# A Mamba-2/GLA trunk: loads alone on the sync queue of the second part, stores on ScalarE's queue

## The chip, the cores and the metric

The kernel runs on one core of a Trainium2 chip. A core has five engines with instruction streams of their own: TensorE (PE, with its weight loads shown as PEld), VectorE (DVE), ScalarE (ACT), GpSimd (POOL) and SyncE (SP). SP and ScalarE can both issue DMAs; a DMA instruction stands in its engine's stream in order, and when it waits for a semaphore, what follows it in that stream waits too. The metric is the device time of one execution in microseconds (us); lower is better.

## The reference, cut to what matters

One decoder layer over 16 meta tokens and 2048 tokens, width 1024: a combined input projection, two branches (a Mamba-2 scan and gated linear attention), sigmoid gates that merge them, an output projection with a residual, and a final norm. The change touches only the last lines:

```python
    branches = jnp.stack([y_ssd.astype(y_gla.dtype), y_gla], axis=2)
    branch_proj = jnp.einsum('blnc,ncd->blnd', branches, w_branch)
    gates = jax.nn.sigmoid(merge_g.reshape(b, l, N_BRANCH, D_MODEL))
    merged = jnp.sum(gates * branch_proj, axis=2)
    return hres + jnp.einsum('bld,de->ble', merged, w_out)
...
    return rmsnorm(h, final_norm_w)[:, N_META:]
```

`merge_g` is the product of the normed input u with 2048 columns of the input weight.

## The kernel before, in words

The **first part** (to about 1556 us) works through four blocks of 512 tokens: projections, the scan, the attention. It leaves u and the two branch outputs y in DRAM, transposed. The **second part** (from about 1557 us) holds the large products: the gates, the two branch projections and the output projection. It works on units of 1024 tokens, so there are seven stages in this order: gate0, br00, br10, gate1, br01, br11, out (br*n**s* is branch *n* of unit *s*). A gate stage has 8 pairs of output tiles, a branch stage 4, the out stage 8.

Each stage multiplies 2x2 blocks in seven products instead of eight (Winograd's scheme). A product is 4 x 3 matmuls of 128x128 by 128x512: every fp32 operand is split into two fp32r parts, and three of the four cross products are added up. The order of products in a stage is written out in `order`: pairs are taken two at a time, and for each p of PS = (1, 2, 6, 7, 5, 3, 4) the product p of both. So 14 products make a round; the whole part has 280.

What belongs to a product:

- **A operands** (weights, or the merged tiles m in out): `load_a` fetches four raw tiles of a pair into `ar` buffers (8) by SP; GpSimd makes the sums (L887 to L890, the last into s4); `prep_a` (L896 ScalarE, L897 VectorE) splits one of the seven into an `a` buffer (7), five products ahead.
- **B operands** (u, y, the out weight, and sums of them): `load_b` fetches a raw tile into a `br` buffer (5) by SP (L870); `prep_b` (L875 ScalarE, L876 VectorE) splits it into `b1` to `b7`. The 28 tiles of the next stage are prepared from 12 products before the stage to 10 after its start.
- **Sums of B**: `make_sums` loads four quarter tiles (L76) into two `io` tiles, subtracts on GpSimd (L80) and stores two tiles (L83). Most are made beside the first part; those of the last unit's branches, 16 pieces, are `late` and made in the second part, one every 9 products from product 14, with their stores on SP.
- **Epilogues**: after products 1, 6 and 5, ScalarE copies the PSUM bank into `sn` (L913); product 6, 5 or 3 then goes on adding to that same bank. After products 2, 5, 4 and 3 `use` finishes an output tile. A gate tile is a tanh on ScalarE (L937), stored to g (L938). A branch tile loads its gate tile g into `io` (8 buffers, L948), adds the snapshot (L930), multiplies (L950); branch 0 stores the result to p (L952), branch 1 loads p (L955), adds (L956) and stores to m (L957). An out tile loads its rows of the input (L969), adds (L971), squares on ScalarE (L975); once both halves of a row are there the norm's factor is formed (L981, L982, L983 on GpSimd), both are scaled (L986) and stored (L987).

All loads and stores of the second part are issued by SP. In the first part TensorE and SP follow the order of the source (`tc.manual_schedule`); in the second part a planner places every engine's instructions, SP's and TensorE's too, by its own costs and the time at which it expects each to be ready. `at(pos, fn)` only says where in the source an action stands: after which product.

Of the kernel before, what the change touches and what calls it, by code (L numbers as in the profile page):

```python
# [40 lines left out]
def trunk_kernel(ctx: ExitStack, tc: tile.TileContext, xm, xmt, w_feat, w_tok, w_zm, w_br, w_o,  # L41
# [30 lines left out]
    def make_sums(pool, tag, nb, braw, sums, j, c, store):  # L72
# [6 lines left out]
        for o, x, y in ((b11, b12, b11), (b12, b22, b12), (b22, b22, b11), (b21, b21, b22)):  # L79
            nc.gpsimd.tensor_tensor(o, x, y, op=ALU.subtract)  # L80
        yield
        for dst, src in zip(sums, pair):
            store.dma_start(dst[j][:, :, cs], src)  # L83

# [770 lines left out]

    class Stage:
# [3 lines left out]
        def __init__(self, name, key, npairs, araw, use):  # L860
            self.name, self.npairs, self.araw, self.use = name, npairs, araw, use
            self.braw, self.sums = sums[key]
            self.b, self.braws, self.a, self.ps, self.snap = {}, {}, {}, {}, {}
# [15 lines left out]
        def load_a(self, n):  # L879
# [5 lines left out]
            a11, a21, a22, a12 = raw(0, 0), raw(1, 0), raw(1, 1), raw(0, 1)  # L885
# [14 lines left out]
        def product(self, n, p):  # L900
# [14 lines left out]
            if p == 2:  # L915
                self.use(n, 0, 0, ps, self.snap[n, 1])
            if p == 5:
                self.use(n, 1, 1, self.ps[n, "b"], self.snap[n, 5])
            if p == 4:
                self.use(n, 1, 0, ps, self.snap[n, 6])  # L920
            if p == 3:
                self.use(n, 0, 1, ps, None)
# [10 lines left out]
    def gate_stage(s):  # L933
        def use(n, i, t, ps, snap):
# [3 lines left out]
            nc.sync.dma_start(g_left[2 * s + t][2 * n + i], th)  # L938
# [5 lines left out]
    def branch_stage(s, nb):  # L944
        def use(n, i, t, ps, snap):
            d, b = 2 * n + i, 2 * s + t
            th = io()
            nc.sync.dma_start(th, g_left[b][nb * 8 + d])  # L948
            x = total(ps, snap)
            nc.vector.scalar_tensor_tensor(th, th, 1.0, x, op0=ALU.add, op1=ALU.mult)  # L950
            if nb == 0:
                nc.sync.dma_start(p_left[b][d], th)  # L952
            else:
                part = io()
                nc.sync.dma_start(part, p_left[b][d])  # L955
                nc.vector.tensor_tensor(part, part, th, op=ALU.add)  # L956
                nc.sync.dma_start(m_left[b][d // 4][:, d % 4], part)  # L957
# [3 lines left out]
                         "p (k c) -> p k c", c=P), use)  # L961

    def out_stage():
        fns, res, ssq = [], {}, {}

        def use(n, i, t, ps, snap):
            r0 = (2 * n + i) * P
            r = res[n, i, t] = io()
            nc.sync.dma_start(r, xm[META + r0:META + r0 + P, t * BLK:(t + 1) * BLK])  # L969
# [6 lines left out]
            if (n, i, 1 - t) in res:  # L976
# [7 lines left out]
                for hf in range(2):  # L984
                    o = res[n, i, hf]
                    nc.vector.scalar_tensor_tensor(o, o, q[:, 0:1], fns[hf], op0=ALU.mult, op1=ALU.mult)  # L986
                    nc.sync.dma_start(out[r0:r0 + P, hf * BLK:(hf + 1) * BLK], o)  # L987
# [3 lines left out]
                     use)  # L991
# [15 lines left out]
    AHEAD, LOAD = 5, 9  # L1007
# [120 lines left out]
```

## Time and profile before

| what | value |
|---|---|
| median of 3 runs (lowest to highest) | 2385.71 us (2382.58 to 2387.7) |
| the profiled execution: first to last instruction | 2382.4 us (the page gives no time around it) |
| TensorE busy | 2264.0 us (95%) |
| VectorE, ScalarE, GpSimd busy | 1571.8, 1187.5, 680.0 us |
| mean granted TensorE clock | 0.976 |
| SP's DMA queue, ScalarE's DMA queue | 452.66 MB, 63.06 MB |
| ScalarE's waits for br loads from 1560 us on, longest | 16.4 us (y), 13.6 us (out weight), 9.4 us (u) |

How to read the rows below. A timeline row has the start in us, the duration in us, the engine, the line of the kernel, the operation, out<-in by the names of the tiles (numbers left out), the shape, and in brackets the idle time before it with what ended it. SPq and ACTq are the instruction streams that issue DMAs. A row of waits reads "who waits <- for whom: us in total, times, longest us". A row of DMA issues has the count, the size and the median us from issue to landing. The window rows have start:end, length, then busy us and (instructions) of each engine. A busy PE overlaps its own matmuls (each row is 0.39 us long, they start 0.23 us apart), so the pace is read from starts.

### The profile page before, as it was taken

The page shows a single profiled execution, that of the slowest core. Times are in us where ns is not written, and L with a number is a line of the kernel's source. Part 1 is how long each engine was busy: PE and PEld are TensorE (multiplying, and loading weights), DVE is VectorE, ACT ScalarE, POOL GpSimd, SP SyncE. Part 2 cuts the span into 40 slices and gives each one's busy share as a digit, 9 for nine tenths or more (in the row PEclk, how much of TensorE's full clock was granted, in tenths as well). Part 3 has the DMA queues.
Part 4 walks back from the last instruction along what each step waited for, and adds up shares of the span by engine and source line. Part 5 has one row for each costly group of instructions (what it writes and reads, how often), then busy time and mean ns, then how long its engine had stood idle before and what let it go on. Part 6 is the DMA issues. An engine that isn't in the chain of part 4 may idle for free. (4 is left out here: it accounts for less than half of the span.)

```text
span 2382.4 us, 36669 instructions
## 1 busy us (share of the span) xinstructions
PE 2264.0 (95%) x12641; PEld 1970.8 (83%) x12641; DVE 1571.8 (66%) x2889; ACT 1187.5 (50%) x2764; POOL 680.0 (29%) x681
## 2 busy tenths in 40 slices
PE   6899999999999999999999999789989999998998
PEld 6889989888889988888989889668877788877786
DVE  4676665676675676676666655764757855786976
ACT  4665655465544455544455534364634445553443
POOL 3343433122222122321122100324433454332431
PEclk8999999999999999999999999789999999999999
DMA  8665875667786676786666654364777965787652
GB/s 271 213 209 193 293 240 190 225 201 235 245 276 184 215 220 220 258 267 199 208 213 212 205 167 143 131 217 136 263 248 264 313 198 173 251 264 225 231 177 106
DMA packets 301547, 518.07 MB, mean 217 GB/s; under 512 B 27696, under 2 KB 143664, under 8 KB 301360
## 3 DMA queue, kind: packets, MB, share of 16 engines
q1 hardware_dynamic: 231856, 452.66, 58.2%
q10 hardware_dynamic: 69504, 63.06, 8.0%
q8 instruction: 99, 1.62, 0.3%
q14 instruction: 88, 0.72, 0.1%
HBM read 368.42 MB, written 147.19 MB: 216 GB/s over the span
## 5 line engine op out<-in xcount | busy, mean ns | idle before, releaser
L177 PE MATMUL pj<-u,whl 128*128 128x512 f32 (+1 forms) x1184 | 447.4, 378 | 9.3 <-ACT g_all L420 3.3
L179 PE MATMUL pj<-u,whl 128*128 128x512 f32 (+1 forms) x1184 | 431.5, 364 | 0.8 <-POOL whl L165 0.8
L178 PE MATMUL pj<-u,whl 128*128 128x512 f32 (+1 forms) x1184 | 430.9, 364 | 0.0
L177 PE MATMUL pj<-whl,u 128*128 128x256 f32 (+1 forms) x992 | 289.9, 292 | 8.7 <-ACT u L282 6.1
L179 PE MATMUL pj<-whl,u 128*128 128x256 f32 (+1 forms) x992 | 284.1, 286 | 1.3 <-DVE u L284 1.3
L177 PE MATMUL psa<-b,a 128*128 128x512 f32 x640 | 255.5, 404 | 30.8 <-ACT sn L913 20.6
L178 PE MATMUL pj<-whl,u 128*128 128x256 f32 (+1 forms) x992 | 283.8, 286 | 0.7 <-POOL whl L165 0.5
L177 PEld LDWEIGHTS pj<-u,whl 128*128 128x128 f32 x1184 | 225.7, 191 | 47.1 <-ACT g_all L420 3.7
L179 PE MATMUL psa<-b,a 128*128 128x512 f32 x640 | 255.8, 400 | 2.3 <-DVE a L897 2.2
L179 PEld LDWEIGHTS pj<-u,whl 128*128 128x128 f32 x1184 | 225.2, 190 | 36.7 <-POOL whl L165 1.1
L178 PE MATMUL psa<-b,a 128*128 128x512 f32 x640 | 255.5, 399 | 0.0
L178 PEld LDWEIGHTS pj<-u,whl 128*128 128x128 f32 x1184 | 225.8, 191 | 33.2
L876 DVE TENSOR_TENSOR b<-br,b 128x512 fp32r<-128x512 f32 x196 | 160.8, 842 | 59.3 <-ACT b L875 58.9
L177 PEld LDWEIGHTS pj<-whl,u 128*128 128x128 f32 x992 | 191.0, 193 | 9.7 <-ACT u L282 6.6
L179 PEld LDWEIGHTS pj<-whl,u 128*128 128x128 f32 x992 | 191.2, 193 | 2.1 <-DVE u L284 2.1
L178 PEld LDWEIGHTS pj<-whl,u 128*128 128x128 f32 x992 | 191.1, 193 | 2.0 <-POOL whl L165 1.6
L897 DVE TENSOR_TENSOR a<-ar,a 128x512 fp32r<-128x512 f32 x160 | 136.2, 855 | 83.1 <-ACT a L896 82.6
L80 POOL TENSOR_TENSOR wr<-wr 128x256 f32<-128x256 f32 x80 | 66.2, 828 | 430.9 <-DMA wr<-y 173.0
L165 POOL TENSOR_TENSOR whl<-wr,whl 128x512 fp32r<-128x512 f32 (+1 forms) x100 | 132.7, 1334 | 191.6 <-ACT whl L164 166.3
L875 ACT ACTIVATE b<-br 128x512 fp32r<-128x512 f32 x196 | 119.8, 627 | 133.4 <-DMA br<-br_t 35.4
L177 PEld LDWEIGHTS psa<-b,a 128*128 128x128 f32 x640 | 124.9, 195 | 61.8 <-ACT sn L913 24.1
L462 DVE SCALAR_TENSOR_TENSOR acc<-cin,hcw,acc 128x512 f32<-128x512 f32 (+1 forms) x192 | 156.3, 814 | 26.8 <-ACT acc L458 26.1
(267 smaller groups left out, 5025.1 us busy)
## 6 DMA issues: line engine op xcount, KB each, us to landing
whl<-k_s SPq DMA_DIRECT2D x96, 512.0 KB, 4.5
whl<-k_g SPq DMA_DIRECT2D x96, 512.0 KB, 4.2
whl<-k_v SPq DMA_DIRECT2D x48, 512.0 KB, 3.9
whl<-k_z SPq DMA_DIRECT2D x36, 512.0 KB, 3.7
wr<-in_w_feat SPq DMA_DIRECT2D x64, 256.0 KB, 4.4
k_s<-whl SPq DMA_DIRECT2D x32, 512.0 KB, 3.5
cb<-cumd ACTq DMA_DIRECT2D x64, 256.0 KB, 5.7
y<-gg ACTq DMA_DIRECT2D x64, 256.0 KB, 4.6
```

The lines of the kernel that those rows point to most:

```text
L80: nc.gpsimd.tensor_tensor(o, x, y, op=ALU.subtract)
L165: nc.gpsimd.tensor_tensor(hl[:, 1], raw, hl[:, 0].bitcast(F32), op=ALU.subtract)
L177: nc.tensor.matmul(ps, sh, mh, start=first, stop=False, **kw)
L178: nc.tensor.matmul(ps, sh, ml, start=False, stop=False, **kw)
L179: nc.tensor.matmul(ps, sl, mh, start=False, stop=last, **kw)
L462: nc.vector.scalar_tensor_tensor(acc, cin[:, k:k + tt], hcw[:, ti, k:k + 1], acc, op0=ALU.mult, op1=ALU.add)
L875: nc.scalar.activation(t[:, 0], raw, AF.Copy)
L876: nc.vector.tensor_tensor(t[:, 1], raw, t[:, 0].bitcast(F32), op=ALU.subtract)
L897: nc.vector.tensor_tensor(t[:, 1], src, t[:, 0].bitcast(F32), op=ALU.subtract)
```

## The change

The second part's source now stands under `manual_schedule` for TensorE and SP, as the first part's does. Stores are collected (`late_store`) and issued by ScalarE's queue after a later product (`store_due`): one product later for epilogue tiles, two for the late sums. `fetch` loads the epilogue's tiles some products ahead of `use`: 3 for branch 0 and out, 2 for branch 1, where it loads g and p. The late sums stand at `spots`: eight pieces in each gate stage, from its product 9 on, one every 5 products, with no stage of their own in the branches. `load_a` stands 7.5 products before product 1 instead of 9, and loads a12 before a21; `load_b` stands 3.2 products before its `prep_b` instead of 4. The arithmetic and the buffers are the same.

```diff
@@ -78,9 +78,18 @@
         (b12, b11), (b22, b21) = [(t[:, 0], t[:, 1]) for t in pair]
         for o, x, y in ((b11, b12, b11), (b12, b22, b12), (b22, b22, b11), (b21, b21, b22)):
             nc.gpsimd.tensor_tensor(o, x, y, op=ALU.subtract)
+        if store is None:
+            for dst, src in zip(sums, pair):
+                late_store(dst[j][:, :, cs], src, 2)
+            return
         yield
         for dst, src in zip(sums, pair):
             store.dma_start(dst[j][:, :, cs], src)
+
+    stores, step_no = {}, [0]
+
+    def late_store(dst, src, lag=1):
+        stores.setdefault(step_no[0] + lag, []).append((dst, src))
 
     def new_sums(name):
         return [[wdram.tile([P, 2, BLK], F32, tag=f"{name}_t{i}_{j}", name=f"{name}_t{i}_{j}", bufs=1)
@@ -853,12 +862,21 @@
     m_left = [[wdram.tile([P, 4, BLK], F32, tag=f"m_{b}_{j}", name=f"m_{b}_{j}", bufs=1) for j in range(2)]
               for b in range(nblk)]
 
+    USES = {2: (0, 0), 5: (1, 1), 4: (1, 0), 3: (0, 1)}
+    store = late_store
+
+    def store_due(i):
+        for k in sorted(k for k in stores if k <= i):
+            for dst, src in stores.pop(k):
+                nc.scalar.dma_start(dst, src)
+
     class Stage:
 
 
 
-        def __init__(self, name, key, npairs, araw, use):
+        def __init__(self, name, key, npairs, araw, use, fetch=None, ahead=0):
             self.name, self.npairs, self.araw, self.use = name, npairs, araw, use
+            self.fetch, self.ahead = fetch, ahead
             self.braw, self.sums = sums[key]
             self.b, self.braws, self.a, self.ps, self.snap = {}, {}, {}, {}, {}
 
@@ -882,7 +900,7 @@
                 nc.sync.dma_start(t, self.araw(n, i, j))
                 return t
 
-            a11, a21, a22, a12 = raw(0, 0), raw(1, 0), raw(1, 1), raw(0, 1)
+            a11, a12, a21, a22 = raw(0, 0), raw(0, 1), raw(1, 0), raw(1, 1)
             s1, s2, s4 = [mk(rpl, [P, 4, P], F32, "as", bufs=6) for _ in range(3)]
             nc.gpsimd.tensor_tensor(s1, a21, a22, op=ALU.add)
             nc.gpsimd.tensor_tensor(s2, s1, a11, op=ALU.subtract)
@@ -912,14 +930,8 @@
                 sn = mk(opl, [P, BLK], F32, "sn", bufs=6)
                 nc.scalar.activation(sn, ps, AF.Copy)
                 self.snap[n, p] = sn
-            if p == 2:
-                self.use(n, 0, 0, ps, self.snap[n, 1])
-            if p == 5:
-                self.use(n, 1, 1, self.ps[n, "b"], self.snap[n, 5])
-            if p == 4:
-                self.use(n, 1, 0, ps, self.snap[n, 6])
-            if p == 3:
-                self.use(n, 0, 1, ps, None)
+            if p in USES:
+                self.use(n, *USES[p], self.ps[n, "b"] if p == 5 else ps, self.snap.get((n, {2: 1, 5: 5, 4: 6}.get(p))))
 
     def io():
         return mk(opl, [P, BLK], F32, "io", bufs=8)
@@ -935,45 +947,56 @@
             x = total(ps, snap)
             th = io() if snap is None else snap
             nc.scalar.activation(th, x, AF.Tanh, scale=0.5)
-            nc.sync.dma_start(g_left[2 * s + t][2 * n + i], th)
+            store(g_left[2 * s + t][2 * n + i], th)
 
         return Stage(f"gate{s}", ("g", s), 8,
                      lambda n, i, j: w_feat[T_GATE + 2 * n + i, :, j * BLK:(j + 1) * BLK].rearrange(
                          "p (k c) -> p k c", c=P), use)
 
     def branch_stage(s, nb):
+        got = {}
+
+        def fetch(n, i, t):
+            d, b = 2 * n + i, 2 * s + t
+            got[n, i, t] = tiles = [io() for _ in range(1 + nb)]
+            nc.sync.dma_start(tiles[0], g_left[b][nb * 8 + d])
+            if nb:
+                nc.sync.dma_start(tiles[1], p_left[b][d])
+
         def use(n, i, t, ps, snap):
             d, b = 2 * n + i, 2 * s + t
-            th = io()
-            nc.sync.dma_start(th, g_left[b][nb * 8 + d])
+            th, *part = got.pop((n, i, t))
             x = total(ps, snap)
             nc.vector.scalar_tensor_tensor(th, th, 1.0, x, op0=ALU.add, op1=ALU.mult)
             if nb == 0:
-                nc.sync.dma_start(p_left[b][d], th)
+                store(p_left[b][d], th)
             else:
-                part = io()
-                nc.sync.dma_start(part, p_left[b][d])
-                nc.vector.tensor_tensor(part, part, th, op=ALU.add)
-                nc.sync.dma_start(m_left[b][d // 4][:, d % 4], part)
+                nc.vector.tensor_tensor(part[0], part[0], th, op=ALU.add)
+                store(m_left[b][d // 4][:, d % 4], part[0])
 
         return Stage(f"br{nb}{s}", ("b", nb, s), 4,
                      lambda n, i, j: w_br[nb * 8 + 2 * n + i, :, j * BLK:(j + 1) * BLK].rearrange(
-                         "p (k c) -> p k c", c=P), use)
+                         "p (k c) -> p k c", c=P), use, fetch, 3 - nb)
 
     def out_stage():
-        fns, res, ssq = [], {}, {}
+        fns, res, ssq, done = [], {}, {}, set()
+
+        def fetch(n, i, t):
+            r0 = (2 * n + i) * P
+            res[n, i, t] = r = io()
+            nc.sync.dma_start(r, xm[META + r0:META + r0 + P, t * BLK:(t + 1) * BLK])
 
         def use(n, i, t, ps, snap):
             r0 = (2 * n + i) * P
-            r = res[n, i, t] = io()
-            nc.sync.dma_start(r, xm[META + r0:META + r0 + P, t * BLK:(t + 1) * BLK])
+            r = res[n, i, t]
+            done.add((n, i, t))
             x = total(ps, snap)
             nc.vector.scalar_tensor_tensor(r, x, 0.5, r, op0=ALU.mult, op1=ALU.add)
             if (n, i) not in ssq:
                 ssq[n, i] = mk(spl, [P, 2], F32, "ssf")
             jk = mk(spl, [P, BLK], BF16, "junk", bufs=1)
             nc.scalar.activation(jk, r, AF.Square, accum_out=ssq[n, i][:, t:t + 1])
-            if (n, i, 1 - t) in res:
+            if (n, i, 1 - t) in done:
                 while len(fns) < 2:
                     fns.append(mk(rpl, [P, BLK], F32, "br", bufs=5))
                     nc.sync.dma_start(fns[-1], fnw[:, (len(fns) - 1) * BLK:len(fns) * BLK].to_broadcast([P, BLK]))
@@ -984,11 +1007,11 @@
                 for hf in range(2):
                     o = res[n, i, hf]
                     nc.vector.scalar_tensor_tensor(o, o, q[:, 0:1], fns[hf], op0=ALU.mult, op1=ALU.mult)
-                    nc.sync.dma_start(out[r0:r0 + P, hf * BLK:(hf + 1) * BLK], o)
+                    store(out[r0:r0 + P, hf * BLK:(hf + 1) * BLK], o)
 
         return Stage("out", ("o",), seq // (2 * P),
                      lambda n, i, j: m_left[(2 * n + i) // 4][j][:, :, (2 * n + i) % 4 * P:((2 * n + i) % 4 + 1) * P],
-                     use)
+                     use, fetch, 3)
 
     stages = []
     for s in range(nsb):
@@ -1004,7 +1027,7 @@
         begins.append(len(order))
         for n in range(0, st.npairs, 2):
             order += [(st, n + i, p) for p in PS for i in range(2)]
-    AHEAD, LOAD = 5, 9
+    AHEAD, LOAD = 5, 7.5
     todo = {}
 
     def at(pos, fn):
@@ -1018,27 +1041,32 @@
         for q in range(28):
             p, j = PS[q // 4], q % 4
             pos = begins[si] - 12 + 0.8 * q if si else -0.99 + 0.2 * (q // 4) if q < 16 else 2 * (q // 4 - 4)
-            at(pos - (4 if si else 0.1), lambda st=st, p=p, j=j: st.load_b(p, j))
+            at(pos - (3.2 if si else 0.1), lambda st=st, p=p, j=j: st.load_b(p, j))
             at(pos, lambda st=st, p=p, j=j: st.prep_b(p, j))
     for i, (st, n, p) in enumerate(order):
+        if p in USES and st.fetch:
+            at(i - st.ahead, lambda st=st, n=n, p=p: st.fetch(n, *USES[p]))
+    for i, (st, n, p) in enumerate(order):
         at(i - AHEAD if i >= AHEAD else -0.95 + 0.1 * i, lambda st=st, n=n, p=p: st.prep_a(n, p))
-    i = 14
-    for key in late:
-        for j in range(4):
-            for c in range(2):
-                gen = make_sums(opl, "io", 8, *sums[key], j, c, nc.sync)
-                for k in range(3):
-                    at(i + 2 * k, lambda gen=gen: next(gen, None))
-                i += 9
+    begun_at = [begins[3 * s] for s in range(nsb)]
+    spots = [g + 9 + 5 * k for g in begun_at for k in range(8)]
+    late_sums = [make_sums(opl, "io", 8, *sums[key], j, c, None) for key in late for j in range(4) for c in range(2)]
+    for pos, gen in zip(spots, late_sums):
+        for k in range(2):
+            at(pos + 2 * k, lambda gen=gen: next(gen, None))
 
     def run(i):
         for _, _, fn in sorted(todo.get(i, []), key=lambda e: e[0]):
             fn()
 
-    run(-1)
-    for i, (st, n, p) in enumerate(order):
-        st.product(n, p)
-        run(i)
+    with tc.manual_schedule(engines={mybir.EngineType.PE, mybir.EngineType.SP}):
+        run(-1)
+        for i, (st, n, p) in enumerate(order):
+            step_no[0] = i
+            st.product(n, p)
+            store_due(i)
+            run(i)
+        store_due(len(order) + 9)
 
 
 def _layout(inputs):
```

## The prediction

> **What bounds the kernel now.** I began with the page (its span and the PE row), went on to the busy time by stage, then to every gap of TensorE after 1557 us, then to the waits of ScalarE and of SP's queue.
>
> ```profile
> span 2382.4 us, 36669 instructions
> ```
> ```profile
> 1557.20:1716.60 159.40, 157.16 (x673) 129.36 (x674) 99.67 (x125) 87.98 (x157) 61.83 (x49) 0.97 0.64 207
> 1716.60:1805.20 88.60, 79.47 (x338) 64.32 (x337) 59.60 (x80) 38.55 (x70) 34.85 (x28) 0.96 0.80 263
> 1805.20:1895.20 90.00, 82.56 (x337) 66.70 (x336) 69.32 (x95) 38.96 (x69) 34.06 (x28) 0.92 0.85 285
> 1895.20:2048.00 152.80, 152.68 (x674) 126.08 (x673) 98.99 (x123) 80.04 (x142) 65.87 (x53) 1.00 0.64 210
> 2048.00:2125.50 77.50, 76.53 (x337) 62.88 (x336) 56.72 (x76) 37.45 (x67) 23.70 (x16) 1.00 0.73 245
> 2125.50:2219.80 94.30, 82.97 (x338) 66.95 (x337) 73.94 (x99) 39.53 (x71) 25.05 (x16) 0.93 0.77 245
> 2219.80:2372.30 152.50, 152.43 (x673) 125.89 (x671) 113.65 (x179) 66.48 (x142) 46.98 (x38) 1.00 0.48 162
> 2372.30:2382.40 10.10, 0.00 (x0) 0.00 (x0) 5.69 (x12) 0.72 (x2) 1.42 (x3) 0.66 0.42 157
> ```
>
> The columns of the second fence are the stretch, its length, then busy time and (instructions) of PE, PEld, VectorE, ScalarE and GpSimd, the granted clock, and the DMA share with GB/s. The rows are the seven stages of the second part in order (gate0, br00, br10, gate1, br01, br11, out) and the tail after the last matmul. The diff touches this part alone.
>
> TensorE's own pace comes from two rows, the first and last of 96 matmuls in a row:
>
> ```profile
> 1754.66 0.39 PE L179 MATMUL psb<-b,a 128*128 128x512 f32 x1
> 1776.20 0.39 PE L179 MATMUL psb<-b,a 128*128 128x512 f32 x1
> 1783.92 0.79 PE L177 MATMUL psa<-b,a 128*128 128x512 f32 x1 [7.33 <-ACT sn L913]
> 1784.51 0.63 PE L178 MATMUL psa<-b,a 128*128 128x512 f32 x1
> 1784.93 0.63 PE L179 MATMUL psa<-b,a 128*128 128x512 f32 x1
> ```
>
> 95 steps in 21.54 us are 0.2267 us a matmul. A product is 12 matmuls, 2.72 us; a stage of 56 products needs 152.3 us, one of 28 needs 76.2. So the stages lose 7.1, 12.4, 13.8, 0.5, 1.3, 18.1 and 0.2 us: **53.4 us, 44.3 of it in br00, br10 and br11**. That is all that ordering can win, besides the 10.1 us tail. After a gap the steps are 0.42 us (1784.51 to 1784.93), so a stall costs more than its gap.
>
> What ends the gaps is ScalarE:
>
> ```profile
> PE psa L177 <- ACT sn L913: 20.6, 7, 7.3
> PE psa L177 <- ACT a L896: 8.2, 3, 4.7
> ```
>
> But ScalarE is at most 55% busy in any stage. Around the longest gap:
>
> ```profile
> 1763.70 0.63 ACT L875 ACTIVATE b<-br 128x512 fp32r<-128x512 f32 x1
> 1780.69 0.63 ACT L875 ACTIVATE b<-br 128x512 fp32r<-128x512 f32 x1 [16.36 <-DMA br<-y]
> 1759.61 1.89 DVE L876 TENSOR_TENSOR b<-br,b 128x512 fp32r<-128x512 f32 x3
> 1775.86 1.44 SPq L870 DMA_DIRECT2D br<-y  x3
> ```
>
> ScalarE stood 16.4 us at the preparation of one B tile (L875), and the copy that TensorE needed (sn, L913) stood behind it. The tile's load was not slow: VectorE had freed br buffers by 1761.5, yet SP issued the load at 1775.86. SP was at other rows of its queue:
>
> ```profile
> SPq L76 <- DMA p<-io: 7.4, 3, 4.0
> SPq L83 <- POOL io L80: 6.6, 4, 2.8
> SPq L948 <- DMA p<-io: 4.9, 3, 3.3
> SPq L948 <- DMA br_t<-io: 3.2, 3, 1.4
> ```
>
> That is 22.1 us of waiting in the 36 us from 1740 to 1776, all about io buffers: loads into them wait for a store to finish, a store waits for GpSimd. The loads of the next stage queue behind. The bound of the three lossy stages is thus SP's order, through ScalarE's.
>
> **The change part by part.**
>
> *Stores leave SP.* 192 stores (64 gate, 32 p, 32 m, 32 out, 32 of late sums) go to ScalarE's queue. Issuing one there costs:
>
> ```profile
> L790 ACTq DMA_DIRECT2D y<-gg x32: 321/326/359, 369.1 to 1556.1; - x32
> L83 ACTq DMA_DIRECT2D br_t<-wr x32: 520/521/545, 800.1 to 1134.5; - x32
> ```
>
> 160 x 0.33 + 32 x 0.52 = 69 us of ScalarE's sequencer. The stage table has ScalarE busy 389 of 815 us, so its idle time covers this; at cover lost it would be 69 us. The waits for the data move too:
>
> ```profile
> SPq L987 <- DVE io L986: 51.2, 20, 18.0
> SPq L83 <- POOL io L80: 34.6, 23, 2.8
> SPq L957 <- DVE io L956: 7.4, 12, 1.9
> SPq L952 <- DVE io L950: 3.9, 5, 1.7
> ```
>
> Without the 18.0 of the very end this is 79.1 us in 59 waits, 1.3 us each. Queued behind a waiting store are A and B preparations (A is made 5 products ahead, 13.6 us) and sn copies. The tightest is the copy after product 5: product 3 adds to the same bank one product later, so 2.72 - 0.6 = 2.1 us of slack; the other copies have three products. A mean wait of 1.3 us passes under that. The store is queued a product after its own, which takes most of the wait away too. Bounds: nothing, and all 79 us. I take 3 us (1 each in gate1, out and gate0), near the lower end, because the longest wait among the last three rows is 2.8.
>
> *Loads in source order.* SP keeps loads only; they wait for a free buffer, not for a result to store. B loads come 3.2 products (8.7 us) before their preparation, A loads 7.5 before product 1, instead of 4 and 9. Landing takes:
>
> ```profile
> ar<-in_w_br SPq DMA_DIRECT2D x64, 256.0 KB, 4.1
> br<-br_t SPq DMA_DIRECT2D x64, 256.0 KB, 4.6
> ...
> br<-in_fnw SPq DMA_DIRECT2D x2, 256.0 KB, 4.9
> ```
>
> So a B load has 4 us to spare. An odd pair's A load has 1.5 products, 4.1 us, before its first preparation: no spare. If it is late ScalarE waits a microsecond, 20 times at most, at a place with no sn copy close; TensorE has the 5 products of lead. Cost 0; without the lead up to 20 us. The order a12 before a21 matches the order in which those buffers come free: nothing. TensorE's order was this one already but for the end of a gate stage and of out, where product 4 of the even pair goes before product 3 of the odd one (here the last four products begin with psa, psb, psa, psb; the new order has psa, psa, psb, psb):
>
> ```profile
> 2363.91 0.39 PE L177 MATMUL psb<-b,a 128*128 128x512 f32 x1
> 2366.40 0.39 PE L177 MATMUL psa<-b,a 128*128 128x512 f32 x1
> ```
>
> Both orders feed the last product alike: nothing, at most one product's epilogue earlier or later.
>
> *Epilogue tiles ahead.* g tiles are fetched 3 products ahead in br00 and br01, 2 in br10 and br11 (with p), residual rows 3 ahead in out. Each io tile lives longer. In the first branch a use holds one tile from 3 before to about 3 after: 6 of 8 buffers when every product has a use. In the second it holds two: g about 3 products, p about 4.5, so 7.5 of 8. SP can still be held there, as it is now in br11:
>
> ```profile
> SPq L955 <- DMA m<-io: 14.3, 7, 4.1
> ```
>
> (2160 to 2202 us: the p load waits for the last m store.) By my count of lives SP runs about 1.2 products late at the worst, 3.3 us against the 4 us that a B load can spare: small stalls, not 7 us ones. br00's exit has one tile a use and no sums: 12.4 becomes 1.5. br10 and br11: 13.8 and 18.1 become 5 each; bounds 0 (as gate1 and out lose) and what they lose now; nearer to the lower end because three of the four waits of 1740 to 1776 are gone from SP (no sums load, no store, and no io buffer that a sum's store holds; the wait of L948 for a p store stays). br01 stays at 1.3.
>
> *Late sums beside gates.* 8 pieces to gate0, 8 to gate1, none in branches. Where GpSimd works, VectorE is slowed:
>
> ```profile
> 2165.57 0.68 DVE L950 SCALAR_TENSOR_TENSOR io<-io,psa 128x512 f32<-128x512 f32 x1
> 1796.36 1.77 DVE L950 SCALAR_TENSOR_TENSOR io<-io,sn 128x512 f32<-128x512 f32 x1
> 1795.96 1.62 POOL L888 TENSOR_TENSOR as<-as,ar 128x512 f32<-128x512 f32 x1
> ```
>
> The Trainium skill, "SBUF — State Buffer", section "Who interferes with whom", says that a VectorE instruction with two SBUF inputs and a GpSimd one that reads SBUF exclude each other for a whole instruction; by that rule the second row could have taken 1.62 + 0.68 = 2.3 us, and the trace has 1.77, so it agrees in kind. The branches are rid of their sums, the gates get them; VectorE is 63 and 65% busy in the gates, which covers it. The first piece now starts at product 9 of gate0, while B preparations still crowd: I add nothing beyond the 1 us above; uncovered it would be a few us.
>
> *Start and tail.* The first loads keep their order: 7.1 stays. The tail's last stores start on ScalarE instead of SP: 10.1 stays.
>
> **Sum**, by stage: 8.1 + 1.5 + 5 + 1.5 + 1.3 + 5 + 1.2 = 23.6 us lost instead of 53.4: 29.8 less. The profiled span 2382.4 becomes 2352.6. The page shows no time around the span; the median of the runs lies 3.3 us above it (2385.7), so 2356.
>
> **The rivals.**
>
> *A: io buffers hold SP as before.* The 7.5 of 8 count speaks for it, and that m stores end SP's waits in br11 now. Then br10 and br11 keep 13.8 and 18.1: loss 45.5, gain 8, 2378. Against it: today's waits include sums and stores that are gone.
>
> *B: ScalarE takes SP's place (slower).* A store waiting for GpSimd or VectorE holds the sn copy of product 5 beyond its 2.1 us. Place: gate stages (stores of sums behind GpSimd) and out (behind L986). Price: half of the 79.1 us reaching TensorE is 39.6, minus the 29.8: 2395.5. It decides from 30 us on, that is when 38% of those waits land on TensorE. For: gate1 and out lose next to nothing now and can only lose. Against: 1.3 us each, and the waits were counted a product earlier than the stores now stand.
>
> *C: nothing, 2386.* SP's issue time was never the bound: the 20 rows of the second part's DMA view, from A loads to the norm weights, count 720 issues, and at the 0.33 to 0.52 us shown they are 240 to 375 of 815 us. Then only the order counts, and if other buffers hold SP as long, nothing is won. The Trainium skill, "DMA: Bandwidth & Descriptors", section "Issuing engines are not separate DMA queues", says so in general: transfers of all queues share the same 16 engines, and a second queue saves issue time alone. By that rule the sum is zero; the trace does not agree here, as the 22.1 us are waits and not issues.
>
> **How the numbers follow.** Forecast 0.64, with its own range 2340 (44 us won) to 2370 (br10 and br11 keep 9 and 12, br00 4); A 0.15; C 0.08; B 0.13. Within 0.2% (4.8 us) no measurement of this kernel could tell it from no change. Faster 0.64 + 0.15 = 0.79, same 0.08, slower 0.13. The range, 2336 to 2380, takes in the forecast, most of A, and below 2340 a start that wins back a part of its 7.1 us.
>
> **What would show it.** Right: matmul groups with under 10 us idle in all; no ScalarE wait for br over 5 us; no store left on SP; the stages near 153, 78, 81, 154, 78, 81 and 153 us. Wrong: ScalarE's queue waiting for VectorE or GpSimd with sn copies behind (B); SP waiting for m or p stores for over 10 us at the ends of br10 and br11 (A).

## The result and the profile after

| | before | after |
|---|---|---|
| median (lowest to highest, runs) | 2384.14 us (2382.54 to 2387.7, 4) | 2359.76 us (2353.16 to 2368.68, 4) |
| ratio after / before, 95% interval | | 0.9898 [0.9875, 0.9922] |
| span of the profiled execution | 2382.4 us | 2351.4 us |
| both kernels again, later | 2383.72 us (11) | 2354.54 us (2347.87 to 2359.4, 5), ratio 0.9875 [0.985, 0.99] |

The change makes the kernel 24.4 us faster; 2356 (2336 to 2380) was forecast. The profiled execution after is the fastest of its four runs (2353.16), 6.6 us under their median. One later run of the kernel before took 3724.27 us at a granted clock of 0.557 and is left out of every comparison.

The page's span, and the two DMA queues that SP and ScalarE issue on (packets, MB, share of 16 engines):

```profile
span 2351.4 us, 36510 instructions
q1 hardware_dynamic: 200112, 402.32, 53.2%
q10 hardware_dynamic: 101248, 113.41, 13.9%
```

50.3 MB have moved from SP's queue to ScalarE's. The busy time by stage, with the columns of the prediction's stage table (gate0, br00, br10, gate1, br01, br11, out, and the tail):

```profile
1555.20:1717.60 162.40, 157.46 (x672) 129.15 (x673) 96.61 (x126) 88.30 (x157) 75.53 (x64) 0.97 0.71 231
1717.60:1793.80 76.20, 76.20 (x338) 63.10 (x337) 60.32 (x78) 38.59 (x68) 24.98 (x16) 1.00 0.73 248
1793.80:1871.50 77.70, 76.41 (x337) 62.99 (x336) 69.88 (x92) 34.81 (x62) 26.41 (x16) 1.00 0.81 272
1871.50:2031.70 160.20, 154.61 (x673) 126.91 (x672) 95.50 (x126) 82.74 (x146) 74.47 (x64) 0.99 0.70 228
2031.70:2108.00 76.30, 76.30 (x338) 63.02 (x337) 57.96 (x78) 38.62 (x68) 24.93 (x16) 1.00 0.73 252
2108.00:2188.70 80.70, 77.72 (x337) 63.93 (x336) 71.73 (x95) 35.54 (x64) 25.76 (x16) 0.98 0.84 270
2188.70:2341.20 152.50, 152.50 (x673) 125.98 (x671) 114.90 (x182) 70.59 (x150) 44.54 (x38) 1.00 0.54 177
2341.20:2351.40 10.20, 0.01 (x1) 0.00 (x0) 5.41 (x12) 0.72 (x2) 1.47 (x2) 0.76 0.42 155
```

Set against TensorE's own pace (152.3 us for a stage of 56 products, 76.2 for one of 28) these rows give the loss of each stage:

| us lost in | gate0 | br00 | br10 | gate1 | br01 | br11 | out | sum |
|---|---|---|---|---|---|---|---|---|
| before | 7.1 | 12.4 | 13.8 | 0.5 | 1.3 | 18.1 | 0.2 | 53.4 |
| forecast | 8.1 | 1.5 | 5 | 1.5 | 1.3 | 5 | 1.2 | 23.6 |
| after | 10.1 | 0.0 | 1.5 | 7.9 | 0.1 | 4.5 | 0.2 | 24.3 |

The sum is as forecast, its parts are not. The four branch stages lost 45.6 us and lose 6.1, half of what was forecast for them; the two gate stages lost 7.6 and lose 18.0. So of the 39.5 us won in the branches 10.4 were given back in the gates. The last matmul comes 31 us earlier, of which 2 are from the first part, which the diff does not touch (this part now starts at 1555.2).

Where the time went in a gate stage: the end of gate0. First TensorE's timeline, then ScalarE's, then SP's queue; last, what SP's queue waited for there.

```profile
1700.26 0.39 PE L188 MATMUL psa<-b,a 128*128 128x512 f32 x1
1705.24 0.80 PE L186 MATMUL psa<-b,a 128*128 128x512 f32 x1 [4.60 <-ACT sn L931]
```
```profile
1696.69 0.62 ACT L914 ACTIVATE a<-ar 128x512 fp32r<-128x512 f32 x1
1703.03 0.63 ACT L893 ACTIVATE b<-br 128x512 fp32r<-128x512 f32 x1 [5.72 <-DMA br<-br_t]
1704.08 0.63 ACT L893 ACTIVATE b<-br 128x512 fp32r<-128x512 f32 x1 [0.42 <-DMA br<-br_t]
1704.61 0.58 ACT L931 ACTIVATE sn<-psa 128x512 f32<-128x512 f32 x1
```
```profile
1687.81 2.38 SPq L888 DMA_DIRECT2D br<-br_t  x3
1690.48 9.09 SPq L900 DMA_DIRECT2D ar<-in_w_br  x4
1699.62 2.32 SPq L888 DMA_DIRECT2D br<-br_t  x5
```
```profile
SPq L900 <- DVE a L915: 5.7, 1, 5.7
```

Read from the bottom up: the four A loads of a pair took SP 9.1 us, 5.7 of them one wait for VectorE to free an `ar` buffer. Five B loads stood behind them and were issued from 1699.6 on. ScalarE had two of their preparations (L893) ahead of the copy that TensorE needed (L931), and stood 5.7 us at the first. TensorE started no matmul for 4.98 us (1700.26 to 1705.24; all gaps below are counted like this, from start to start), and restarted at half pace. It is the chain of the kernel before (a late B load, a waiting preparation, the copy behind it) at another place and with another cause: not a store or an `io` buffer held SP, but an A load issued before its buffer was free. The end of gate1 looks the same: four A loads take 9.3 us from 2004.21, five B loads follow at 2013.59, ScalarE waits 6.25 us, and TensorE's gap of 4.80 us ends at 2019.31.

### The profile page after: what moved, and what is told of

The parts are those of the page before. It is cut to its first block, busy times and chain, and to the rows that moved or that the text cites. A ratio compares the mean times of both kernels' runs of the same rounds, so it can differ in the third digit from the quotient of the medians.

```text
span 2351.4 us, 36510 instructions
## 1 busy us (share of the span) xinstructions
PE 2251.5 (96%) x12641; PEld 1963.8 (84%) x12641; DVE 1563.5 (66%) x2889; ACT 1187.9 (51%) x2764; POOL 680.9 (29%) x681
## 4 chain that ended last, share of the span: by engine, by line
PE 47%; DMA 7%; DVE 6%; ACT 3%; issue 2%; SPq 1%; POOL 1%; ACTq 0%; DVEq 0%; POOLq 0%
PE pj L186 6%; PE pj L188 6%; PE pj L187 6%; PE psa L186 4%; PE psa L188 4%; PE psa L187 4%; PE psb L188 2%; PE psb L186 2%; PE psb L187 2%; DMA br<-br_t 1%; PE psc L188 1%; PE psc L186 1%; PE psc L187 1%; DVE a L915 1%; PE pc L690 1%
## 5 line engine op out<-in xcount | busy, mean ns | idle before, releaser
L186 PE MATMUL pj<-u,whl 128*128 128x512 f32 (+1 forms) x1184 | 447.0, 378 | 10.1 <-ACT g_all L429 3.3
L186 PE MATMUL psa<-b,a 128*128 128x512 f32 x640 | 253.1, 396 | 16.7 <-ACT sn L931 14.8
L187 PE MATMUL psa<-b,a 128*128 128x512 f32 x640 | 251.7, 393 | 0.0
L188 PE MATMUL psa<-b,a 128*128 128x512 f32 x640 | 251.4, 393 | 0.0
L915 DVE TENSOR_TENSOR a<-ar,a 128x512 fp32r<-128x512 f32 x160 | 151.2, 952 | 77.8 <-ACT a L914 77.3
L80 POOL TENSOR_TENSOR wr<-wr 128x256 f32<-128x256 f32 x80 | 68.6, 857 | 426.0 <-DMA wr<-y 173.4
L894 DVE TENSOR_TENSOR b<-br,b 128x512 fp32r<-128x512 f32 x196 | 149.1, 783 | 43.8 <-ACT b L893 43.6
L905 POOL TENSOR_TENSOR as<-ar,ar 128x512 f32<-128x512 f32 x40 | 55.0, 1374 | 421.5 <-DMA ar<-in_w_br 140.0
L893 ACT ACTIVATE b<-br 128x512 fp32r<-128x512 f32 x196 | 119.0, 626 | 95.0 <-DMA br<-br_t 38.1
```

The lines of the kernel that those rows point to most:

```text
L186: nc.tensor.matmul(ps, sh, mh, start=first, stop=False, **kw)
L187: nc.tensor.matmul(ps, sh, ml, start=False, stop=False, **kw)
L188: nc.tensor.matmul(ps, sl, mh, start=False, stop=last, **kw)
L893: nc.scalar.activation(t[:, 0], raw, AF.Copy)
L894: nc.vector.tensor_tensor(t[:, 1], raw, t[:, 0].bitcast(F32), op=ALU.subtract)
L905: nc.gpsimd.tensor_tensor(s1, a21, a22, op=ALU.add)
```

## The experiments

The loss by stage in all kernels (worked out as above, to about 0.3 us; each from one profiled execution) is the table that the rest refers to:

| kernel | gate0 | br00 | br10 | gate1 | br01 | br11 | out | sum |
|---|---|---|---|---|---|---|---|---|
| stores back on SP | 8.1 | 4.5 | 13.5 | 5.1 | 8.6 | 15.3 | 4.9 | 60.0 |
| SP by the planner | 7.2 | 1.4 | 6.7 | 0.0 | 5.5 | 5.5 | -0.2 | 26.1 |
| sums at old places | 8.4 | 1.7 | 9.2 | 8.0 | 1.6 | 6.4 | -0.3 | 35.0 |
| fetch at use | 11.2 | 4.1 | 4.4 | 7.8 | 6.0 | 3.4 | 5.1 | 42.0 |
| before, stores on ScalarE | 3.8 | 8.2 | 9.7 | 2.0 | -0.2 | 8.3 | 0.0 | 31.8 |
| before, sums at gates | 6.3 | 4.5 | 14.9 | 0.0 | 5.2 | 14.8 | -0.3 | 45.4 |
| A load in two halves | 8.0 | 0.0 | 6.8 | 11.5 | 0.0 | 7.6 | 2.9 | 36.8 |
| stores without delay | 9.9 | 0.0 | 4.5 | 7.4 | 0.0 | 4.8 | -0.3 | 26.3 |
| ScalarE in source order too | 4.2 | 0.0 | 6.3 | 1.5 | 0.0 | 5.0 | 6.2 | 23.2 |
| TensorE and ScalarE in source order | 8.9 | 0.0 | 1.4 | 1.9 | 0.0 | 0.1 | 4.5 | 16.8 |
| the change again | 12.2 | 0.0 | 1.9 | 7.7 | 0.0 | 5.2 | -0.3 | 26.7 |
| TensorE and ScalarE in source order, again | 8.8 | 0.0 | 2.0 | 2.7 | 0.0 | 4.1 | 4.6 | 22.2 |

In all of them but the three with ScalarE in source order the planner still places ScalarE's instructions, in the two made from the kernel before TensorE's and SP's too, and it places them anew for every edit; a stage's loss can move by some us through that alone ("the change again" is the same kernel as the change: 26.7 against 24.3). The first four ran on one chip (before: 2384.6, 14 runs), the next four on a second (2383.1, 21), then two on a third (2386.71, 7) and the last two on a fourth (2383.72, 11).

### The change with its stores back on SP

```diff
             for dst, src in stores.pop(k):
-                nc.scalar.dma_start(dst, src)
+                nc.sync.dma_start(dst, src)
```

> The changed kernel with one thing undone: the collected stores are issued by SP again, at the same late places in the source. Theory 1 (a store on SP that waits for its tile holds the loads behind it): much of the gain goes, 2370 to 2390 us, with SP waiting over 40 us for VectorE, ScalarE and GpSimd tiles at stores and ScalarE standing over 5 us at br loads at the ends of br00, br10 and br11. Rival (the order and the distance made the gain, not the queue): within 6 us of the changed kernel, about 2354 to 2366 us.

Measured: 2389.54 us (2381.76 to 2397.03, 10 runs), ratio 1.0025 [1.0008, 1.0041]. The whole gain is gone, and a little more. SP's queue waits of this kernel from 1556 us on, in source order with the stores in it:

```profile
SPq L871 <- ACT sn L949: 97.3, 34, 6.7
SPq L871 <- DVE io L970: 93.4, 25, 8.6
SPq L871 <- DVE io L974: 83.0, 28, 6.5
SPq L871 <- DVE io L1009: 80.5, 20, 19.3
```

With the waits for GpSimd (33.0) and for L949's other tiles (12.1), SP stands 399 us at stores (L871) whose data are not there yet. This sum tells where SP stands and is no price: the kernel before stands some 130 us at its stores, and is 5 us faster. The loads behind them land late, and ScalarE and TensorE wait for those:

```profile
ACT b L893 <- DMA br<-br_t: 73.1, 51, 4.4
```
```profile
PE psa L186 <- ACT sn L931: 37.9, 20, 5.2
```

In this kernel and in the change SP issues the same loads in the same order, and TensorE's matmuls are in the same order too. The loads do not travel longer beside the stores: from issue to landing the median is 4.5 us for the B tiles of `br_t` and 5.4 for the A tiles of the branches, against 4.8 and 5.2 in the change. So it is not a second queue that makes loads faster; they are issued later when stores stand ahead of them. The stores' place is necessary for the gain; source order, early fetches and the new places of the sums win nothing without it.

### The change with SP placed by the planner

```diff
-    with tc.manual_schedule(engines={mybir.EngineType.PE, mybir.EngineType.SP}):
+    with tc.manual_schedule(engines={mybir.EngineType.PE}):
```

> The changed kernel with SP's order left to the planner again (TensorE alone in source order). Theory 1 (what matters is which instructions SP holds, less their exact order): 2352 to 2370 us, and the two 5 us gaps at the ends of the gate stages change, since they come from SP's fixed order (A loads ahead of B loads). Rival (source order is what makes the gain): 2375 us or more.

Measured: 2354.83 us (2351.05 to 2356.87, 4), ratio 0.9875 [0.9854, 0.9896]: no slower than the change. Here the planner issues the B loads first at the end of gate0, and the A loads one by one between them, so no B load stands behind a long wait at an `ar` buffer (the longest of 1685 to 1705 us is 0.9 us):

```profile
1686.01 8.89 SPq L888 DMA_DIRECT2D br<-br_t  x8
1695.28 0.33 SPq L900 DMA_DIRECT2D ar<-in_w_br  x1
```

ScalarE's longest wait for a B tile there is 0.97 us. gate0 has no gap at its end, and gate1 loses nothing instead of 7.9, but br10, br01 and br11 lose 17.7 together instead of 6.1. SP's source order thus moves the loss from branches to gates; it adds nothing to the sum that these runs can tell.

### The change with the late sums at their old places

```diff
-    spots = [g + 9 + 5 * k for g in begun_at for k in range(8)]
+    spots = [14 + 9 * k for k in range(16)]
```

> The changed kernel with the late sums at their old places (one piece every 9 products from product 14, through br00 and br10). Theory 1 (in the branches the sums hold io buffers and slow VectorE through GpSimd): br00 and br10 lose 4 to 12 us more, 2362 to 2374 us. Rival (the sums cost nothing wherever they are once stores are off SP): within 4 us of the changed kernel. Both: the two gaps of about 5 us at the ends of gate0 and gate1 stay, as they have nothing to do with the sums; if they go, the sums made them.

Measured: 2362.04 us (2361.07 to 2367.83, 4), ratio 0.9912 [0.989, 0.9934], not told apart from the change (0.9898). gate1 still loses 8.0, so the sums beside the gates are not what costs the gates their time. Its profiled execution loses 10.7 more than the change's, 7.7 of it in br10, but it is also the slowest of its runs.

### The change with fetches right at their use

```diff
             if p in USES:
+                if self.fetch:
+                    self.fetch(n, *USES[p])
...
-        if p in USES and st.fetch:
+        if False:
```

> The changed kernel with the epilogue's tiles loaded at their use instead of 2 or 3 products ahead. Theory 1 (a load of 4.5 us then stands between product and epilogue, but io buffers are held for a shorter time): VectorE waits for io loads, a few us a branch stage, 2360 to 2375 us. Rival (PSUM banks have the slack, and shorter lives help SP): 2350 to 2360 us.

Measured: 2371.75 us (2365.89 to 2376.17, 6), ratio 0.9942 [0.9922, 0.9962]: 12 us slower than the change at the medians, 17 slower than the change's second set of runs. SP's waits for an `ar` buffer, 100.9 us with 11.6 as the longest in the change, are now:

```profile
SPq L900 <- DVE a L915: 169.2, 35, 17.4
```

Behind such a wait now stands the load of a tile that is due at once, and br00, br10, br01 and out lose 3 to 6 us more each. (The way from there to each of TensorE's gaps was not followed.) The wait that was expected, VectorE at the loads of g and p, is not there; its longest for a tile of the epilogue is 2.1 us, at a residual row. So with SP in source order about half of the gain rests on the early fetch. With SP placed by the planner the gain is there without it, as the next kernel shows.

### The kernel before, with its stores on ScalarE's queue and nothing else changed in the source

```diff
-            nc.sync.dma_start(g_left[2 * s + t][2 * n + i], th)
+            nc.scalar.dma_start(g_left[2 * s + t][2 * n + i], th)
...
-                gen = make_sums(opl, "io", 8, *sums[key], j, c, nc.sync)
+                gen = make_sums(opl, "io", 8, *sums[key], j, c, nc.scalar)
```

(and the same for p, m and out)

> The kernel before with one part alone: the second part's stores are issued by ScalarE at their old places; order, distances, sums and planner as before. Theory 1 (stores on SP are the main cause): a large share of the gain, 2355 to 2372 us. Rival (the queue is needed but does not suffice, since the io loads at their use still hold SP): 2375 to 2388 us. Since loads at the use cost 12 us in the changed kernel, I expect the upper half of the first range.

Measured: 2358.01 us (2352.7 to 2368.12, 6), ratio 0.9901 [0.987, 0.9932]. That is the change's whole gain, from 192 DMAs with another issuing engine. (The planner placed all engines anew for it; the stores put back on SP, above, is the comparison in which the order of loads and matmuls is the same.) SP's queue now waits above all for free buffers. Two rows of its waits from 1556 us on, for A and for B loads, first of the kernel before, then of this one:

```profile
SPq L882 <- DVE a L897: 132.0, 89, 5.5
SPq L870 <- DVE b L876: 81.7, 90, 25.9
```
```profile
SPq L882 <- DVE a L897: 221.6, 102, 11.9
SPq L870 <- DVE b L876: 112.8, 124, 26.7
```

SP is ahead of its loads: 334 us at buffers that VectorE has still to free, 214 before. ScalarE's waits for the y tiles, whose longest was the 16.4 us of the prediction, shrink with it:

```profile
ACT b L875 <- DMA br<-y: 5.4, 4, 2.4
```

### The kernel before, with its late sums beside the gates

```diff
-    i = 14
-    for key in late:
...
+    spots = [begins[3 * s] + 9 + 5 * k for s in range(nsb) for k in range(8)]
```

> The kernel before with one part alone: the late sums beside the gate stages, stores still on SP. Theory 1 (the sums are a small part: 24 of the 64 GpSimd operations leave br00 and br10, and SP's waits L76 and L83 go with them): br00 and br10 lose 5 to 10 us less, br11 as before, 2374 to 2382 us. Rival (the sums are what held SP there): br00 and br10 lose under 6 us together, 2365 us or less.

Measured: 2377.56 us (2372.67 to 2390.47, 10), ratio 0.9988 [0.9965, 1.001]: no difference that can be told, with the interval from 8 us won to 2 lost. In its one profile br00 loses 4.5 instead of 12.4 and br01 5.2 instead of 1.3; br10 and br11 still lose 14.9 and 14.8. Taking the sums out of the branches does not free SP while the stores of products are still on it.

### The change with each A load in two halves

```diff
-            a11, a12, a21, a22 = raw(0, 0), raw(0, 1), raw(1, 0), raw(1, 1)
+            a11, a12 = raw(0, 0), raw(0, 1)
+            self.a[n] = {1: a11, 2: a12}
+            yield
+            a21, a22 = raw(1, 0), raw(1, 1)
```

The second half, with its GpSimd sums, comes two products later.

> The changed kernel with the A load in two steps: a11 and a12 as now, a21 and a22 with their sums two products later, when VectorE has freed their buffers. Theory 1 (the 5 us gaps at the ends of gate0 and gate1 come from SP standing at the last A load with five B loads behind it): both gaps go or shrink under 2 us, gate0 and gate1 together lose 6 to 10 us less, 2346 to 2354 us. Rival (the B loads are late for another reason, as in br11): the gaps stay, 2356 to 2364 us.

Measured: 2369.15 us (2364.74 to 2380.27, 10), ratio 0.9952 [0.9929, 0.9975]: slower than the change. SP's hold at the end of gate0 did go:

```profile
1688.30 3.63 SPq L900 DMA_DIRECT2D ar<-in_w_br  x4
```

9.09 us became 3.63, and the gap at the gate's end shrank with it (4.98 to 3.57 us, at 1706.26; 4.80 to 2.65 at the end of gate1). That supports the chain read above. But the two gates together lose 19.5 us and not less, against the expectation: GpSimd got its operands later, and in gate1 this came up:

```profile
1905.81 0.54 ACTq L871 DMA_DIRECT2D br_t<-io  x1
1906.39 0.60 ACT L934 ACTIVATE sn<-psa 128x512 f32<-128x512 f32 x1 [7.39 <-POOL io L80]
```
```profile
1897.94 1.30 POOL L908 TENSOR_TENSOR as<-ar,ar 128x512 f32<-128x512 f32 x1 [16.80 <-DMA ar<-in_w_feat]
```

GpSimd stood until 1897.9 for an A tile, so the late sum (L80) behind it was late, its store on ScalarE's queue waited, and the sn copy (L934 here) stood 7.4 us behind that store; TensorE's gap of 5.21 us ends at 1907.05. This is rival B, at one place: a store that waits for GpSimd holds the copy. It is shown here to be real. In the change no gap over 1 us has such a store in its chain.

### The change with its stores without delay

```diff
-    def late_store(dst, src, lag=1):
+    def late_store(dst, src, lag=0):
```

> The changed kernel with epilogue stores right after their product instead of one later. Theory 1 (the planner places a store on ScalarE by the time it expects its tile, so the product's delay matters little): within 5 us of the changed kernel, 2353 to 2365 us, and io buffers come free a little sooner. Rival (without the delay ScalarE waits for VectorE in front of sn copies): 2368 us or more, with gaps in out and the gates.

Measured: 2356.23 us (2355.26 to 2358.39, 4), ratio 0.9891 [0.9859, 0.9923]: as the change. The product's delay of a store does no measurable work.

### The change with ScalarE in source order too, and with ScalarE but not SP

```diff
-    with tc.manual_schedule(engines={mybir.EngineType.PE, mybir.EngineType.SP}):
+    with tc.manual_schedule(engines={mybir.EngineType.PE, mybir.EngineType.SP, mybir.EngineType.Activation}):
```

> The changed kernel with ScalarE, too, in source order in the second part (an sn copy then stands before the B preparations of later products, which the planner had put ahead of it). Theory 1 (the gaps at the ends of gate0, gate1 and br11 come from B preparations that the planner placed in front of an sn copy, trusting loads that were late): these gaps of 3 to 5 us go, 2340 to 2350 us. Rival (a fixed order makes ScalarE stand at stores and preparations at other places): 2358 to 2380 us, with waits of ScalarE for VectorE and GpSimd tiles over 100 us.

Measured: 2356.16 us (2350.64 to 2358.65, 4), ratio 0.9868 [0.9841, 0.9894]. If the gates lose because preparations stand ahead of the copy, the source's order must mend that, and it does: gate0 loses 4.2 instead of 10.1, gate1 1.5 instead of 7.9. The copy at the end of gate0 now waits for TensorE, not the other way round:

```profile
1702.56 0.60 ACT L931 ACTIVATE sn<-psa 128x512 f32<-128x512 f32 x1 [3.92 <-PE psa L188]
```

But br10 and out lose 6.3 and 6.2 (1.5 and 0.2), and ScalarE now waits for VectorE's results in order:

```profile
ACT sn L949 <- DVE sn L942: 79.0, 44, 5.7
ACT a L914 <- DVE io L970: 59.6, 19, 5.4
```

In the change these two rows are 17.3 and 14.5 us. The second row is ScalarE standing at stores ahead of its preparations. The waits come out about even with what the gates gain, and the 2340 to 2350 us expected did not come. (TensorE's longest waits are now for VectorE's half of a B tile, L894, 9.4 us in all, in three waits; the way there from ScalarE's waits was not followed.)

With TensorE and ScalarE in source order and SP by the planner (`engines={PE, Activation}`):

> TensorE and ScalarE in source order, SP left to the planner. Theory 1 (what counts is that no sn copy stands behind a late B tile; SP's order counts little): 2340 to 2352 us, within 5 us of the kernel with SP in source order too. Rival (ScalarE in source order loses at stores): 2358 to 2380 us.

Measured: 2352.02 us (2346.81 to 2356.23, 4), ratio 0.9853 [0.983, 0.9877], the lowest median so far, with 16.8 us lost. A second pair of runs sets it beside the change on one chip:

> The changed kernel as it is, beside the next one on the same chip, to compare the two directly: 2353 to 2368 us as before, ratio 0.986 to 0.993.

> The kernel with TensorE and ScalarE in source order and SP left to the planner, beside the changed kernel on the same chip. If its 2352 us was its own: 2346 to 2356 us, 4 us or more under the changed kernel. Rival (the difference was that of two chips): within 3 us of the changed kernel.

Measured: the change 2354.54 us (2347.87 to 2359.4, 5), ratio 0.9875 [0.985, 0.99]; the other 2352.05 (2343.05 to 2363.52, 6), ratio 0.9869 [0.9842, 0.9896]. They are not told apart. No version is shown to beat the change.

### What the experiments say together

| medians, us | stores on SP | stores on ScalarE |
|---|---|---|
| SP placed by the planner | 2385 (before) | 2358 (before + stores), 2355 (change, SP by planner) |
| SP in source order | 2390 (change, stores on SP) | 2360, 2355 (the change, twice) |

Down a column nothing is won; from left to right some 25 to 35 us, in either row. The stores are the change; the rest is neutral, or undoes a harm of SP's source order (the early fetch).

## Why the prediction was right, point by point

- **What bound the kernel** (SP held at stores and `io` buffers, through ScalarE's order): right, and shown from both sides, by the stores back on SP (2389.5) and by the stores alone on ScalarE (2358.0).
- **"Stores leave SP", 3 us on ScalarE:** the waits did move. ScalarE's idle time behind stores, by the tile that was last (VectorE's L970 and L974, GpSimd's L80), is 69.8 us in the change, where 79.1 was forecast from SP's rows. The three longest rows:

```profile
ACT a L914 <- DVE io L970: 14.5, 9, 2.0
ACT a L914 <- DVE io L974: 12.1, 6, 5.5
ACT sn L949 <- POOL io L80: 11.0, 4, 5.0
```

  They cost less than the 3 us: out loses 0.2, as before, and none of TensorE's gaps over 1 us has a waiting store in its chain. The reason given, that the delay of a product takes most of the wait away, was not needed (2356.2 without it).
- **"br00's exit 12.4 becomes 1.5; br10 and br11 5 each":** right in direction, too cautious: 0.0, 1.5 and 4.5. What is left is br11's exit, a gap of 3.37 us until 2176.4. ScalarE stands at a B tile of the out weight, whose load SP issued behind the four m tiles of an A load, 5.8 us before ScalarE could go on (5.3 us is the median landing time of these loads):

```profile
2161.88 2.72 SPq L900 DMA_DIRECT2D ar<-m  x4
2164.70 1.65 SPq L888 DMA_DIRECT2D br<-out_t  x1
2170.53 0.63 ACT L893 ACTIVATE b<-br 128x512 fp32r<-128x512 f32 x1 [4.93 <-DMA br<-out_t]
```

  So the load was issued late. From 2150 to 2170 us SP stood 4.6 us at `br` buffers (five waits for VectorE's L894) and at most 1.7 us at an `io` buffer. Which of these, or the m tiles ahead, made it late no run tested.

- **"If it is late ScalarE waits a microsecond … Cost 0" (the A load of an odd pair):** this is the step that failed. It asked whether the A load comes too late for its own preparation. It comes too early for its buffer: SP waits 5.7 us at it, and what is queued behind it on SP, five B loads, is what ScalarE stands at. Price: the gap and the slow restart, about 6.3 us in gate0 and most of the 7.9 in gate1, where 0 was taken. The planner for SP (gate1 0.0) and ScalarE in source order (1.5) each take the gap away.
- **"Late sums beside gates", 1 us in gate0; A and B order, TensorE's order, tail:** nothing in the runs against them. With the sums at their old places gate1 loses 8.0 as well, and the tail is 10.2 us (10.1). "7.1 stays" at the start did not hold as a number: of gate0's 10.1 some 6.3 are at its end, so the start cost 3.8; in the other kernels gate0 lost 3.8 to 12.2. What sets the start is open.
- **The sum** was right by luck, because two errors cancelled: branches 12.8 forecast and 6.1 measured, gates 9.6 and 18.0. The second profile of the change has the same parts (7.1 and 19.9), so they are not one run's. The step from span to median (3.3 us) was too small for this sample: 8.4, of which some 1.8 lie outside the span (2353.16 against 2351.4 in the profiled run) and 6.6 are what the profiled run was faster than the median.
- **The signs.** Right: no store is left on SP, the rows of the stores are all on ScalarE's stream (the largest kind below), and the branch stages and out take what was said or less.

```profile
L871 ACTq DMA_DIRECT2D g<-sn x48: 322/327/1353, 1571.4 to 2033.6; - x48
```

  Wrong: the matmul groups stand 16.7 us and not under 10, ScalarE waits over 5 us for a br load three times, and the gates take 162 and 160 us instead of 153 and 154. The failed step has most of it: its two gaps are 9.0 of the 16.7 us, and two of the three waits are its own (5.7 and 6.3 us; the third, 5.1 us, is at the end of br10). The 153 us for gate0 did not fit the prediction's own sum, which has 152.3 + 8.1 = 160.4 there.

```profile
PE psa L186 <- ACT sn L931: 14.8, 7, 4.6
PE psa L186 <- ACT b L893: 1.9, 1, 1.9
```
```profile
ACT b L893 <- DMA br<-br_t: 38.1, 24, 6.2
```

- **The rivals.** A (buffers hold SP as before) did not come: ahead of br11's gap SP's longest wait at an `io` buffer is 1.7 us. B did not reach TensorE in the change, and does in gate1 of the kernel with split A loads. C (nothing is won) fell. The Trainium skill, "DMA: Bandwidth & Descriptors", section "Issuing engines are not separate DMA queues", says that starting DMAs from several engines saves issue time alone; the runs here do not agree, since with the stores on SP it stands 399 us at stores that wait for data, and holds the loads behind them for as long. The issue time of the 192 stores left SP as well, and no run tells its share of the 25 us apart (2383.1 to 2358.0 us with only the stores moved).

Open are the start of gate0, and whether the last 17 to 27 us lost can be had: each order of SP and ScalarE that was tried loses them at other places. Runs of one kernel on one chip differ by up to 20 us (the kernel before 2374 to 2394 on the second chip, the last kernel 2343 to 2364 on the fourth), so orders a few us apart are not told apart here.

## What to carry to other kernels

Look at what an engine's DMA queue stands at before asking how much it issues: a store that waits for a result is a lock on every load behind it, and moving the stores to an engine whose own work comes after those results can be the whole gain of a rewrite. When a step is moved on a queue, ask two questions of it, not one: is it in time for its user, and is its buffer free when the queue reaches it, since being early costs those behind it. Undo or do alone each part of a bundled change; here one edit of engine names did the work of all.

## What the runs showed of the hardware

A long stall of TensorE costs more than its gap. After the 4.98 us gap at the end of gate0 the matmuls started 0.60 us apart, 0.42 to 0.43 five times over, 0.35, then 0.23 again; the eight steps from the restart took 3.31 us instead of 1.81. In the kernel before, a shorter gap had a longer tail, and a later one (some rows of the timeline):

```profile
2136.18 0.39 PE L179 MATMUL psc<-b,a 128*128 128x512 f32 x1
2138.97 0.50 PE L177 MATMUL psa<-b,a 128*128 128x512 f32 x1 [2.41 <-ACT sn L913]
...
2140.01 0.60 PE L178 MATMUL psa<-b,a 128*128 128x512 f32 x1
2140.40 0.63 PE L179 MATMUL psa<-b,a 128*128 128x512 f32 x1
...
2142.96 0.62 PE L179 MATMUL psa<-b,a 128*128 128x512 f32 x1
2143.39 0.43 PE L177 MATMUL psa<-b,a 128*128 128x512 f32 x1
```

After a gap of 2.79 us four steps came at nearly full pace, and only from 2140.0 to 2143.4, a microsecond after the restart, were the steps 0.39 to 0.43 us. So the slow stretch need not begin with the restart. Over all the profiled executions, with the 16 steps behind each gap added up: every gap of 3.7 us or more had 1.5 to 2.8 us on top; gaps of 2.2 to 3.6 us had either 0.1 to 0.3 or 1.5 to 3.0; gaps of 1.6 to 2.2 us had 0.1 to 0.6. What decides between the two in the middle group is open.
